# Where tiles lie in SBUF: a streaming encoder on one core, with the tiles that TensorE does not stream placed first

## The chip, the core and the metric

The kernel runs on one core of a Trainium2 chip. The metric is the device time of one execution in microseconds (us). The core has a matrix engine (TensorE, PE in the profile; its weight loads are PEld), three engines for elementwise work (VectorE is DVE, ScalarE is ACT, GpSimd is POOL) and queues that start DMA transfers (SyncE is SP). They share a scratch memory of 128 partitions, SBUF. A tile takes the same bytes of every partition, so its place is one number: the byte offset within a partition. TensorE reads two operands from SBUF for each matmul: the stationary one (128 by 128, brought in by a weight load) and the moving one (streamed through, up to 512 columns here). It writes to a separate memory, PSUM.

## The reference, cut to what matters

Input and output are 512 tokens of width 1024 in float32. The network has two layers:

```python
def reference(x, ...):
    h = x
    for layer in range(DEPTH):                      # DEPTH = 2
        if layer == N_A_LAYERS:                     # 1
            k_nope, k_rope, v = mla_shared_kv(h, ...)
        hn = rms_norm(h, mix_pre_g[layer])
        if layer < N_A_LAYERS:
            m = conformer_conv(hn, ...)             # 1024->2048, gate, 31-tap conv, norm, 1024->1024
        else:
            m = mla_attention(hn, ..., k_nope, k_rope, v, cos, sin)
        h = h + rms_norm(m, mix_post_g[layer])
        f = squared_relu_mlp(rms_norm(h, ffn_pre_g[layer]), w_ff1[layer], w_ff2[layer])   # 1024->4096->1024
        h = h + rms_norm(f, ffn_post_g[layer])
    return h
```

Most of the arithmetic is in the matrix products of the two MLPs. The kernel forms each float32 product from three products of a reduced type (fp32r): every operand is split into a high part and a low part, and high by high, low by high and high by low are added up in PSUM.

## The kernel before, in words

**Weights.** A block of weights (128 by up to 1024 columns, 512 KB) is loaded by the SP queue into a tile of the ring `raw` (5 places of 4 KB per partition). ScalarE writes its high part into a tile of the ring `wh` (5 places of 4 KB), VectorE the low part into a tile of the ring `wl` (6 places of 4 KB). TensorE then uses `wh` and `wl`. This is `weight` (L731) and `split` (L789). The rings `raw`, `wh` and `wl` are handed out in the order of first use (`fifo=True`): a block takes whichever place came free first.

**Two kinds of product.** In `products` (L768: both `ff1` matrices, the first convolution matrix, the latents) the weights are stationary and the activations move: in the profile this reads `mm<-big,wh`, the moving tile first and the stationary tile second. In `by_tokens` (L878: second convolution matrix, attention output) and `product` within `feed_forward` (L1001: `ff2`, by Strassen's seven products) the activations are stationary and the weights move: `mm<-wh,big`. A block of `ff1` is 24 matmuls of 512 columns: 8 slices of the inner dimension, each with `wh`, `wl`, `wh` as the stationary tile.

**Activations** and everything else of 2 KB per partition are in the pool `big` (48 places) and `tmp` (5 places). The residual stream `h` (4 tiles of 4 KB), the rows of gains and biases `row` (2 places of 4 KB), the vectors `vt`, the small statistics `stat`, a scratch target `junk`, the identity matrix `ident` and the averaging matrices `col` make up the rest. TensorE also reads `h` and `stat` (as stationary operands in transposes and in broadcasts), `ident` and `col` (as moving operands), in float32 and 128 columns at a time.

**Order of the work.** The program is recorded first and then scheduled by a planner (`Program`, L284) with a cost table in nanoseconds. The planner knows tiles by their ring and place number. It knows nothing of addresses.

**Addresses.** A place of a ring gets its address when its tile is first made (`Tag.make`, L208). `Tag.__init__` makes place 0 at once, where the ring is declared; the other places are made when the first instruction that uses them is issued, after planning. So in the kernel before, place 0 of every ring and all single tiles come first, in the order of their declarations, and places 1 and up follow in the order of use.

Of the kernel before, what the change touches and what calls it, by code (L numbers as in the profile page):

```python
# [8 lines left out]
F32 = mybir.dt.float32  # L9
# [5 lines left out]
P = 128  # L15
T = 512
D = 1024
# [4 lines left out]
TB = T // P  # L22
# [22 lines left out]
NVEC = _n  # L45
# [598 lines left out]
def trunk(ctx: ExitStack, tc: tile.TileContext, xT, xN, wts, vec, along, rope, cw, out):  # L644
# [6 lines left out]
    def tag(name, n, shape, where=pool, fifo=False):  # L651
        tags.append(Tag(where, name, n, shape, fifo))
        return tags[-1]

    def one(name, shape):
        return nc.tile(tag(name, 1, shape))

    RAW = tag("raw", 5, [P, D], fifo=True)
    WH = tag("wh", 5, [P, D], fifo=True)
    WL = tag("wl", 6, [P, D], fifo=True)  # L660
    BIG = tag("big", 48, [P, T])
    TMP = tag("tmp", 5, [P, T])
    MM = tag("mm", 6, [P, T], psum, fifo=True)
    BC = tag("bc", 2, [P, T], psum, fifo=True)
    STAT = tag("stat", 8, [P, 24])
    ROW = tag("row", 2, [P, D])

    JUNK = one("junk", [P, T])

    def big(dt=F32):  # L670
        return nc.tile(BIG, dt)
# [5 lines left out]
        return nc.tile(TMP)  # L677


    vt = one("vt", [P, NVEC])  # L680
    n = VEC["mix_pre0"] + KT
    nc.scalar.dma_start(out=vt[:, :n], in_=vec[:, :n])
    nc.sync.dma_start(out=vt[:, n:], in_=vec[:, n:])
# [12 lines left out]
    for k in range(KT):  # L696
        nc.sync.dma_start(out=xf[k], in_=xT[k])

    h = [one(f"h{b}", [P, D]) for b in range(TB)]
    ident = one("ident", [P, P])  # L700
    nc.gpsimd.memset(ident, 0.0)
    done = nc.gpsimd.affine_select(
        out=ident, in_=ident, compare_op=ALU.not_equal, fill=1.0, base=0, pattern=[[-1, P]], channel_multiplier=1
# [27 lines left out]
    def weight(key):  # L731

        while key not in blocks:
            name, parts = USE[len(blocks)]
            i, n = BLK[parts[0][0]], _cols[BLK[parts[0][0]]]
            if name[0] in GAINS:
                blocks[name] = scaled(name, wts[i])
                continue
            raw, hi, lo = nc.tile(RAW), nc.tile(WH, F32R), nc.tile(WL, F32R)
            step = 256 if i < 2 else n  # L740
            for o in range(0, n, step):
                nc.sync.dma_start(out=raw[:, o : o + step], in_=wts[i, :, o : o + step])
            for other, sign in parts[1:]:
                if sign > 0:
                    nc.gpsimd.dma_start(out=raw, in_=wts[BLK[other]], accum_op=ALU.add)
                else:
                    second = nc.tile(RAW)
                    nc.sync.dma_start(out=second, in_=wts[BLK[other]])
# [96 lines left out]
    def sums(parts, t0, dim):  # L845


        sm = nc.tile(BC)
        for i, (o, src, b) in enumerate(parts):

            nc.tensor.matmul(
                sm[:, o * P : (o + 1) * P], lhsT=src[:, t0 + b * P : t0 + (b + 1) * P], rhs=cols[dim],
                start=(i == 0), stop=(i == len(parts) - 1),
            )
        return sm.rearrange("p (o k) -> p o k", k=P)[:, :, 0]

    def rsqrt_bc(accs, t0, n, dim, eps, dst=None):

        nb = n // P
        sm = sums([(b, acc, b) for acc in accs for b in range(nb)], t0, dim)  # L860
        st = nc.tile(STAT)
        var = st[:, :nb]
# [8 lines left out]
    def row(name):  # L871
        t = nc.tile(ROW)
        nc.early = 30000.0
        nc.sync.dma_start(out=t, in_=along[ROWS.index(name)])
        nc.early = 0.0
        return t
# [28 lines left out]
    def residual(F, g, b, dh, o, st, on, r2):  # L905


        nc.scalar.activation(
            JUNK, F[b][dh], AF.Square, scale=1.0 / 32 if r2 is None else r2[:, b : b + 1], accum_out=st[:, o : o + 1]
        )  # L910
# [21 lines left out]
    def prenorm(X, g, t, r=None):  # L932

        t0, n = t
        for kk in range(KT // 2):
# [5 lines left out]
            for j in range(2):  # L941
# [4 lines left out]
                else:  # L946
                    split_scaled(pt, v(g, k), src, X[k], d)
        st = nc.tile(STAT)
        for i, b in enumerate(HALVES[t]):
            for dh in range(2):  # L950
                o = 16 + 2 * i + dh
                nc.scalar.activation(
                    JUNK, h[b][:, dh * DH : (dh + 1) * DH], AF.Square, scale=1.0 / 32, accum_out=st[:, o : o + 1]
                )
# [108 lines left out]
    def post_norm(gen, F, g, then, groups, r2=None, last=False):  # L1063
# [3 lines left out]
        for b, dh in gen:  # L1067
            bs = group[b]
            if not seen[bs]:
                st[bs] = nc.tile(STAT)  # L1070
            if last:
# [121 lines left out]
    for c in range(KT):  # L1193
# [29 lines left out]
        if c == 5:  # L1223

            hold = h + [nc.tile(ROW)]
            for b, t in enumerate(hold):
# [32 lines left out]
    for t0, n in (HA, HB):  # L1259
        s, nb = slice(t0, t0 + n), n // P  # L1260
        nc.scalar.activation(sq[:, s], CO[last][:, s], AF.Square)
        sm = sums([(o + b, a, b) for o, a in ((0, xs), (nb, acc), (0, CO[last]), (nb, sq)) for b in range(nb)], t0, D)
        st = nc.tile(STAT)
        mean, d2, var = st[:, 16 : 16 + nb], st[:, 20 : 20 + nb], st[:, 0:nb]
# [73 lines left out]
    def latent(name, g, dst, t, dim):  # L1338
# [12 lines left out]
        sm = sums([(b, acc, b) for b in range(nb)], t0, dim)  # L1351
        st = nc.tile(STAT)
        var, a = st[:, :nb], st[:, 12 : 12 + nb]
# [76 lines left out]
    nc.scalar.activation(undealt(r1n, FULL), dealt(r1), AF.Copy)  # L1430
    st = nc.tile(STAT)
    var, r = st[:, :TB], st[:, 16 : 16 + TB]
# [263 lines left out]
```

## Time and profile before

| what | value |
|---|---|
| time, 3 runs | 1065.81 us median (1065.62 to 1068.2) |
| span of the profiled execution | 1066.7 us, 0.9 us above that median |
| PE busy | 1045.5 us (98%), 5284 matmuls |
| PEld, DVE, ACT, POOL busy | 884.7, 764.1, 640.9, 141.6 us |
| DMA | 204.08 MB, mean 191 GB/s |
| granted TensorE clock, mean over the span | 0.993 |

A line of groups of instructions reads: source line, engine, operation, tile written, tiles read, partitions by elements and type, count, then the busy time in us and the mean duration of one in ns, then the time that the engine was idle before them and what ended it. Nearly all instructions stand at L640, the one line that issues what the planner has ordered; the tile names tell them apart. A view of stages has for each stretch its length, the busy time of each engine with the number of its instructions, the granted clock, the mean busy share of the DMA engines and what they moved. Successive matmuls overlap, so the duration of one is longer than the time from the start of one to the start of the next.

The profile does not show addresses. They are in the built program, and its matmuls stand in the same order as the trace's 5284 records, so each record can be given the addresses of its two operands. The offsets in the built program before, below 76 KB (bytes within a partition; the first 16 KB are the DMA queues' scratch area):

```
     0  DMA scratch (16384)    37088  junk (2048), 39136 vt (1460), 40608 warm
 16512  raw  place 0 (4096)    40640  h (4 tiles of 4096)
 20608  wh   place 0 (4096)    57024  ident, col (3), meanmat (512 each)
 24704  wl   place 0 (4096)    59584  uu (3 tiles of 2176)
 28800  big  place 0 (2048)    66112  r2, wq (16 each)
 30848  tmp  place 0 (2048)    66208  big (2048)
 32896  stat place 0 (96)      68256  raw (4096)
 32992  row  place 0 (4096)    72352  big (2048), and so on
```

The other places of `raw`, `wh`, `wl`, `big` and `tmp` and the second `row` lie above 65536 (64 KB): `wh` at 96928, 148128, 168608, 180896; `wl` at 109216, 154272, 162464, 172704, 176800.

### The profile page before, as it was taken

Reading aid. Unit: us, or ns where it says so; the run is one execution under the profiler, and the core shown is the slowest. Engines: PE = TensorE matmul, PEld = TensorE weight load, DVE = VectorE, ACT = ScalarE, POOL = GpSimd, SP = SyncE. Lnnn points to the kernel's source line nnn. Section 1 sums busy time; section 2 is a strip of 40 time slices with the busy share of each in tenths; the row PEclk is TensorE's granted clock in tenths of the full one; section 3 lists DMA queues with packets and bytes.
Section 4 is the critical chain, followed back from the end, with each engine's and each line's share of the span. In section 5 each row is a group of like instructions: output and inputs, shape, how many; then the busy total and the mean of one; then the engine's idle time right before and its main releaser. Section 6 shows DMA issues by size and latency. Waiting matters only on the chain. (4 is left out here: it accounts for less than half of the span.)

```text
span 1066.7 us, 15181 instructions
## 1 busy us (share of the span) xinstructions
PE 1045.5 (98%) x5284; PEld 884.7 (83%) x5284; DVE 764.1 (72%) x1559; ACT 640.9 (60%) x1343; POOL 141.6 (13%) x165
## 2 busy tenths in 40 slices
PE   8989999999999999999999999999999999999996
PEld 7878988988888888888888888889888888888885
DVE  6497994857438737959988987547574495497698
ACT  8543497766545446545767877558565554454652
POOL 1110011100100100001104533301010010000010
PEclk9989999999999999999999999999999999999998
DMA  9995888657866848658923132557599388485684
GB/s 288 300 254 171 287 211 236 156 168 207 253 171 190 257 126 241 189 182 227 237 69 93 56 100 81 174 182 179 161 245 253 112 235 257 143 243 168 187 237 129
DMA packets 67613, 204.08 MB, mean 191 GB/s; under 512 B 7632, under 2 KB 13904, under 8 KB 67536
## 3 DMA queue, kind: packets, MB, share of 16 engines
q1 hardware_dynamic: 49680, 150.15, 40.9%
q0 software_dynamic: 13536, 49.29, 25.6%
q10 hardware_dynamic: 4320, 3.68, 1.1%
q8 instruction: 41, 0.67, 0.3%
q14 instruction: 36, 0.29, 0.1%
HBM read 197.58 MB, written 5.51 MB: 190 GB/s over the span
## 5 line engine op out<-in xcount | busy, mean ns | idle before, releaser
L640 PE MATMUL mm<-big,wh 128*128 128x512 f32 (+1 forms) x1512 | 441.1, 374 | 1.2 <-ACT wh L640 1.2
L640 PE MATMUL mm<-wh,big 128*128 128x512 f32 (+1 forms) x1216 | 374.7, 387 | 0.0
L640 ACT ACTIVATE wh<-raw 128x512 fp32r<-128x512 f32 (+2 forms) x444 | 251.0, 612 | 117.7 <-PE mm L640 73.8
L640 PEld LDWEIGHTS mm<-big,wh 128*128 128x128 f32 x1512 | 275.6, 188 | 52.4 <-ACT wh L640 1.5
L640 DVE TENSOR_TENSOR wl<-raw,wh 128x512 fp32r<-128x512 f32 (+1 forms) x356 | 227.7, 680 | 106.5 <-ACT wh L640 104.1
L640 PE MATMUL mm<-big,wl 128*128 128x512 f32 (+1 forms) x756 | 282.5, 374 | 0.0
L640 PEld LDWEIGHTS mm<-wh,big 128*128 128x128 f32 x1216 | 226.3, 188 | 46.9
L640 PE MATMUL mm<-wl,big 128*128 128x512 f32 (+1 forms) x608 | 234.9, 387 | 0.1
L640 PEld LDWEIGHTS mm<-big,wl 128*128 128x128 f32 x756 | 142.6, 189 | 25.7 <-DVE wl L640 0.5
L640 PEld LDWEIGHTS mm<-wl,big 128*128 128x128 f32 x608 | 114.2, 188 | 23.4 <-DVE wl L640 0.2
L640 POOL DMA_DIRECT2D raw<-wts x64 | 55.5, 867 | 572.7 <-DMA raw<-wts 190.4
L640 ACT ACTIVATE big<-tmp 128x256 f32<-128x256 f32 (+1 forms) x208 | 95.9, 493 | 43.2 <-DVE tmp L640 37.3
L640 DVE TENSOR_TENSOR big<-big,big 128x512 f32<-128x512 f32 (+4 forms) x103 | 69.8, 698 | 55.9 <-ACT big L640 55.6
L640 ACT ACTIVATE tmp<-mm 128x512 f32<-128x512 f32 (+1 forms) x75 | 41.7, 556 | 103.1 <-PE mm L640 102.0
L640 PE MATMUL mm<-big,big 128*128 128x256 f32 (+3 forms) x520 | 83.5, 310 | 1.8 <-DVE big L640 1.8
L640 PEld LDWEIGHTS mm<-big,big 128*128 128x128 f32 x520 | 73.1, 189 | 7.0 <-DVE big L640 2.3
L640 ACT ACTIVATE big<-mm 128x512 f32<-128x512 f32 (+5 forms) x106 | 56.6, 537 | 33.9 <-PE mm L640 32.9
L640 DVE TENSOR_TENSOR big<-tmp,big 128x512 fp32r<-128x512 f32 (+1 forms) x96 | 60.9, 642 | 15.3 <-ACT big L640 12.7
L640 DVE SCALAR_TENSOR_TENSOR big<-big,vt,big 128x512 fp32r<-128x512 f32 (+29 forms) x95 | 63.3, 736 | 8.0 <-ACT big L640 8.0
L640 DVE TENSOR_TENSOR big<-big,mm 128x512 f32<-128x512 f32 x96 | 63.7, 683 | 3.2 <-PE mm L640 2.8
L640 DVE TENSOR_TENSOR tmp<-big,big 128x512 f32<-128x512 f32 x80 | 53.3, 686 | 8.9 <-ACT big L640 8.9
L640 POOL DMA_DIRECT2D wl<-wts x30 | 26.1, 869 | 213.0 <-ACT wl L640 113.3
(90 smaller groups left out, 775.9 us busy)
## 6 DMA issues: line engine op xcount, KB each, us to landing
raw<-wts SPq DMA_DIRECT2D x222, 512.0 KB, 5.0
raw<-wts POOLq DMA_DIRECT2D x64, 512.0 KB, 7.9
wl<-wts POOLq DMA_DIRECT2D x30, 512.0 KB, 8.4
big<-cw SPq DMA_DIRECT2D x45, 256.0 KB, 5.6
big<-wts SPq DMA_DIRECT2D x12, 256.0 KB, 4.3
row<-along SPq DMA_DIRECT2D x5, 512.0 KB, 5.5
raw<-wts SPq DMA_DIRECT2D x12, 192.0 KB, 2.7
big<-xT SPq DMA_DIRECT2D x8, 256.0 KB, 4.2
```

The lines of the kernel that those rows point to most:

```text
L640: return f(*args, **kwargs)
```

## The change

The declarations are put in another order, and all places of `raw` and `row` are made at once. After it the built program has, from the bottom:

```
     0  DMA scratch (16384)    47232  h (4 tiles of 4096)
 16512  raw  place 0 (4096)    63616  vt (1460)
 20608  row  place 0 (4096)    65088  stat place 0 (96)
 24704  raw  places 1 to 4     65184  ident (512)
 41088  row  place 1           65696  wh place 0, 69792 wl place 0
 45184  junk (2048)            73888  big place 0, 75936 tmp place 0
```

`col`, `meanmat`, `uu` and every place of `wh`, `wl`, `big` and `tmp` are above 65536 now. The built programs have the same instructions in the same order on every engine, with the same shapes, ring places and semaphores; addresses alone differ. The second half of the diff takes the old declarations out.

```diff
     RAW = tag("raw", 5, [P, D], fifo=True)
+    ROW = tag("row", 2, [P, D])
+    for t in (RAW, ROW):
+        for place in range(1, t.count):
+            t.make(f"{t.name}_", F32, place)
+    JUNK = one("junk", [P, T])
+    h = [one(f"h{b}", [P, D]) for b in range(TB)]
+    vt = one("vt", [P, NVEC])
+    STAT = tag("stat", 8, [P, 24])
+    ident = one("ident", [P, P])
     WH = tag("wh", 5, [P, D], fifo=True)
     WL = tag("wl", 6, [P, D], fifo=True)
     BIG = tag("big", 48, [P, T])
     TMP = tag("tmp", 5, [P, T])
     MM = tag("mm", 6, [P, T], psum, fifo=True)
     BC = tag("bc", 2, [P, T], psum, fifo=True)
-    STAT = tag("stat", 8, [P, 24])
-    ROW = tag("row", 2, [P, D])
-
-    JUNK = one("junk", [P, T])
...
-    vt = one("vt", [P, NVEC])
...
-    h = [one(f"h{b}", [P, D]) for b in range(TB)]
-    ident = one("ident", [P, P])
```

## The prediction

> **What bounds the kernel now.** I read the page's busy times first, then the stages, then what the matrix engine waits for.
>
> ```profile
> span 1066.7 us, 15181 instructions
> ...
> PE 1045.5 (98%) x5284; PEld 884.7 (83%) x5284; DVE 764.1 (72%) x1559; ACT 640.9 (60%) x1343; POOL 141.6 (13%) x165
> ```
>
> ```profile
> 0.00:50.00 50.00, 47.20 (x205) 38.55 (x206) 28.08 (x52) 33.86 (x63) 6.78 (x22) 1.00 0.98 293
> 50.00:100.00 50.00, 46.31 (x228) 39.66 (x227) 42.00 (x64) 23.09 (x48) 5.18 (x6) 0.93 0.84 226
> ...
> 250.00:300.00 50.00, 50.00 (x221) 41.09 (x220) 28.10 (x46) 30.87 (x59) 6.04 (x7) 1.00 0.90 245
> 300.00:350.00 50.00, 50.00 (x220) 41.03 (x219) 33.34 (x55) 28.30 (x56) 3.45 (x4) 1.00 0.63 178
> ```
>
> ```profile
> PE mm L640 <- DMA uu<-dealt: 3.7, 1, 3.7
> PE mm L640 <- DVE big L640: 1.8, 3, 0.7
> PE mm L640 <- POOL big L640: 1.6, 1, 1.6
> PE bc L640 <- DVE big L640: 1.5, 3, 0.7
> PE mm L640 <- ACT wh L640: 1.2, 1, 1.2
> ```
>
> In the MLP stages (two of them above) TensorE is busy 50.00 of 50.00 us: the next matmul is always ready, and the stage lasts as long as its matmuls take to follow each other. Its waits are few: 3.7 us once for a DMA, and 1.2 us in all for split weights. So the pace of the matmuls is the time, and an edit that moves no instruction can act only through that pace, or by making another engine or the DMAs slow enough to be waited for. The matmuls that carry the load are 512 columns wide:
>
> ```profile
> L640 PE MATMUL mm<-big,wh 128*128 128x512 f32 x1256 | 394.7, 393 | 1.2 <-ACT wh L640 1.2
> L640 PE MATMUL mm<-wh,big 128*128 128x512 f32 x1152 | 361.1, 392 | 0.0
> L640 PE MATMUL mm<-big,wl 128*128 128x512 f32 x628 | 246.3, 392 | 0.0
> L640 PE MATMUL mm<-wl,big 128*128 128x512 f32 x576 | 225.9, 393 | 0.0
> ```
>
> That is 3612 of the 5284. The question is whether they all follow each other at one pace. Four successive blocks of `ff1`, 24 matmuls each, cut at their first matmuls:
>
> ```profile
> 963.59:969.14 5.55, 5.55 (x25) 4.50 (x24) 5.55 (x10) 1.16 (x2) 0.86 (x1) 1.00 0.55 206
> 969.14:974.74 5.60, 5.60 (x25) 4.50 (x24) 5.60 (x11) 3.16 (x6) 0.00 (x0) 1.00 0.84 187
> 974.74:980.19 5.45, 5.45 (x25) 4.51 (x24) 4.36 (x8) 3.29 (x7) 0.00 (x0) 1.00 0.26 92
> 980.19:985.63 5.44, 5.44 (x25) 4.51 (x24) 1.90 (x3) 2.88 (x6) 0.00 (x0) 1.00 0.40 142
> ```
>
> They don't: the same work, TensorE never idle, the clock at 1.00, and 5.55, 5.60, 5.45, 5.44 us. By the built program the first block has `wl` in place 0 (offset 24704) and `wh` higher up; the second has `wh` in place 0 (20608) and `wl` higher up; the third and fourth have both above 64 KB. A change of pace within one stretch, at the matmul, in the timeline (start, duration):
>
> ```profile
> 1000.14 0.39 PE L640 MATMUL mm<-big,wl 128*128 128x512 f32 x1
> 1000.37 0.61 PE L640 MATMUL mm<-big,wh 128*128 128x512 f32 x2
> 1000.82 0.39 PE L640 MATMUL mm<-big,wl 128*128 128x512 f32 x1
> 1001.05 0.61 PE L640 MATMUL mm<-big,wh 128*128 128x512 f32 x2
> 1001.50 0.39 PE L640 MATMUL mm<-big,wl 128*128 128x512 f32 x1
> 1001.73 0.63 PE L640 MATMUL mm<-big,wh 128*128 128x512 f32 x2
> 1002.20 0.40 PE L640 MATMUL mm<-big,wl 128*128 128x512 f32 x1
> 1002.43 0.63 PE L640 MATMUL mm<-big,wh 128*128 128x512 f32 x2
> 1002.89 0.39 PE L640 MATMUL mm<-big,wl 128*128 128x512 f32 x1
> 1003.13 0.63 PE L640 MATMUL mm<-big,wh 128*128 128x512 f32 x2
> 1003.59 0.40 PE L640 MATMUL mm<-big,wl 128*128 128x512 f32 x1
> ```
>
> Three matmuls take 0.68 us up to the `wl` at 1001.50, and 0.70, 0.69, 0.70 us from there. At 1001.96, by the program, a block begins that has both `wh` and `wl` in place 0. Paired over the whole trace, record by record with the program's addresses, the 3594 steps from one fp32r matmul of 512 columns to the next that are no stall (under 300 ns) read:
>
> ```
> step from one 512-column matmul to the next     steps   median   mean
> its own or the next one's operand below 64 KB    1097   233 ns   232.39 ns
> none, but one within three matmuls                535   227 ns   228.72 ns
> none near                                        1962   227 ns   227.39 ns
> the same between 256-column matmuls: below 64 KB   184   118 ns   119.39 ns; none near 436, 120 ns, 124.81 ns
> ```
>
> It makes no difference which operand lies low: with the moving one alone low in both of two successive matmuls the mean is 232.1 ns (84 steps), with the stationary one alone 233.9 ns (218 steps). Only three tiles make up nearly all of the first row: `wh`, `wl` and `big`, place 0, at 20608 to 30848. Steps whose moving tile starts at 66208, just above 64 KB, are at the fast pace (53 steps, mean 227.1 ns).
>
> **The change part by part.** *The streamed tiles leave the lowest 64 KB.* Of the 512-column matmuls 726 read at least one such tile (474 `wh`, 203 `wl`, 47 `big`, 2 `meanmat`); the ring sizes say nearly the same, (1256 + 1152) / 5 + (628 + 576) / 6 = 682 for the weights. The gain: 1097 × (232.39 − 227.39) = 5.5 us for the steps that touch one, and 535 × (228.72 − 227.39) = 0.7 us for their neighbours, 6.2 us. The lower bound leaves the neighbours out, 5.5. The upper bound takes as the fast pace not the 227.39, which includes steps at the borders of blocks and of smaller matmuls, but the last block above, 5.44 / 24 = 226.7 ns: 1097 × 5.7 + 535 × 2.0 = 7.3 us. I take 6.2. The blocks agree: 0.11 us for `wl` alone (8 of 24 matmuls), 0.16 for `wh` alone (16 of 24), so 10 to 14 ns for each matmul that touches, and 726 × 10 = 7.3 as well.
>
> The 256-column steps show no penalty, and the float32 ones of 128 columns cost 109 to 112 ns in the median with the moving tile low or high; both count nothing.
>
> *What does not reach the end.* Up to 67 us the pace is not TensorE's alone: DMA engines are 0.98 busy in the first 50 us, and the one long wait ends at 67.3 us with a DMA (`uu<-dealt`, 3.7 us above). About 0.4 us of the gain falls before it, by the same pairing. The transfer is started by work that follows TensorE, so some of it would arrive earlier, but it queues behind loads that do not; the bounds are 0 and 0.4, and I take 0.4 as lost. After that the waits in the table are each for an engine that works on TensorE's own results, so they move with it.
>
> *All `raw` and `row` places and `h` share the lowest 64 KB.* ScalarE and VectorE read `raw`, and the DMAs write it. Before, one place of five was low, so the price is in the trace, paired the same way:
>
> ```
>                                               tile low              tiles high
> ACT wh<-raw 512 columns, raw low or high      620 ns (58)           617 ns (276)
> DVE wl<-raw,wh 512 columns, raw low or high   685.5 ns (46)         685 ns (188)
> load of raw, 512 KB, issue to landing         5.07 us (45 loads)    4.43, 5.12, 5.48, 5.17 us by place (42 to 46 loads each)
> ```
>
> (medians, counts in brackets, `wh` and `wl` high). The 3 ns of ScalarE times its 444 splits is 1.3 us of an engine that is 60% busy and 28 to 31 us of 50 in the stages above; it lies beside TensorE and the sum has 0 for it. The cover is the ring: TensorE waited 1.2 us for ScalarE's `wh` in the whole run. Without that cover the 1.3 us would be the price; I keep it in the range.
>
> *Sum.* −6.2 + 0.4 = −5.8 us: 1066.7 becomes 1060.9 for the profiled execution. That execution is 0.9 us above the median of the runs, so the time is 1065.8 − 5.8 = 1060.0 us. The ends: −7.3 with nothing lost, 1058.5; −5.5 + 0.4 + 1.3 = −3.8, 1062.0.
>
> **The rivals.** *No change (chance 0.08): 1065.8 us.* The slow steps go with something that keeps company with the three tiles, not with where they lie, and it goes with them to 65696 and up, where they now begin. For it: all three are place 0 of their ring, so address and place number are not told apart by them. Against it: in the planner a place is only a number, an address at 66208 is fast, and the slow pace holds for moving and stationary tiles, for three kinds of tile and in all stages. A page speaks for this rival: the Trainium skill, "SBUF — State Buffer", section "Who interferes with whom", says that the only contention on the engines' side is the port pair that VectorE and GpSimd share and that TensorE never waits on anyone; by that rule a tile's place could not matter and the time would stay at 1065.8. This case's trace does not agree, by the 232.39 against 227.39 ns above.
>
> *The gain is caught by the weights (0.05): about 1062.8 us.* Where loads pace the stage, faster matmuls only wait longer for `wh`. The stretch 250 to 300 us has DMA engines 0.90 busy. If half of the stretches were so close to their supply, half of the gain would go: −3. Against it stands the 1.2 us of waiting for `wh`, in one single wait.
>
> *Slower (0.04): about 1070 us.* One mechanism: all 512 KB loads now land in one 64 KB region, where ScalarE and VectorE read at the same time. If that made loads slower, the first 67 us, with DMA engines 0.98 busy, would stretch by as much. It decides from 5.8 / 67 = 9% on; at 15% it adds 10 us, 1060.0 + 10 = 1070. For it: a fifth of the loads landed there before, all of them do now, so the trace has no case of full concentration. Against it: the low place's loads took 5.07 us, amid the others, and ScalarE's reads there cost 3 ns.
>
> **How the numbers follow.** The forecast has 0.83. The range takes its bounds, 1058.5 to 1062.0, and some 0.7 us below and 1.2 us above for what the runs shown differ by (0.2 us between the two lowest, 2.4 us to the highest) and for the third case: 1057.8 to 1063.2. It leaves out the no-change and the slower case, 0.12. A measurement of this kernel can tell about 0.3% from no change, 3.2 us. Faster by more than that: the forecast and a part of the third case, 0.84; within it: no change, the rest of the third case and the forecast's upper tail, 0.12; slower 0.04.
>
> **What would show it.** Right: the 512-column steps are at 226 to 228 ns in nearly all blocks of `ff1`, each 5.44 to 5.46 us, whatever ring place they have; the means of the four groups fall from 392 to 393 towards 390 ns; PE busy falls by about 6 us while the MLP stages keep 50.00 of 50.00; the wait for `uu<-dealt` is 3.7 to 4.2 us. Wrong: some blocks still take 5.55 to 5.60 us (no change), PE's waits for `wh` grow from 1.2 us to several (caught by the weights), or the median time of the `raw` loads from issue to landing rises, with waits on DMA in the first 70 us (slower). The forecast also fails if the half-speed clock, which the 0.93 of the stage from 50 to 100 us shows once, comes a second time.

## The result and the profile after

Measured side by side on one chip, six executions each: the kernel before took 1064.8 us in the median (1063.29 to 1068.2), the changed one 1060.64 us (1058.01 to 1061.76). The ratio is 0.9959, with a 95% interval of 0.9943 to 0.9975, so the change gains 2.7 to 6.1 us. A repetition on another occasion is the first experiment below.

The page of the changed kernel, the span and the busy times:

```profile
span 1058.4 us, 15181 instructions
...
PE 1037.9 (98%) x5284; PEld 883.2 (83%) x5284; DVE 763.0 (72%) x1559; ACT 641.6 (61%) x1343; POOL 141.5 (13%) x165
```

TensorE is busy 7.6 us less for the same 5284 matmuls (1045.5 before), and no other engine moves by as much. The same four blocks of `ff1` that the prediction showed, and the one with both weights in place 0 (start and end, length, busy time of PE, PEld, DVE, ACT and POOL with their instructions, clock, DMA share, GB/s):

```profile
956.16:961.60 5.44, 5.44 (x26) 4.51 (x25) 5.44 (x10) 1.16 (x2) 0.00 (x0) 1.00 0.64 223
961.60:967.04 5.44, 5.44 (x26) 4.51 (x25) 5.44 (x10) 3.16 (x6) 0.86 (x1) 1.00 0.70 135
967.04:972.48 5.44, 5.44 (x26) 4.51 (x25) 4.76 (x8) 3.29 (x7) 0.00 (x0) 1.00 0.40 130
972.48:977.92 5.44, 5.44 (x26) 4.51 (x25) 1.89 (x3) 2.89 (x6) 0.00 (x0) 1.00 0.48 172
994.24:999.68 5.44, 5.44 (x26) 4.51 (x25) 4.56 (x8) 3.82 (x8) 1.73 (x2) 1.00 0.94 285
```

Before, the first four took 5.55, 5.60, 5.45, 5.44 us, and the fifth 5.60 (24 matmuls at 233.3 ns):

```profile
1001.96:1007.56 5.60, 5.60 (x26) 4.50 (x25) 4.40 (x7) 3.81 (x8) 1.72 (x2) 1.00 0.97 267
```

Now all are 5.44, whatever ring place they use. The groups of 512-column matmuls, by shape (busy us, mean ns of one, idle time before):

```profile
L640 PE MATMUL mm<-big,wh 128*128 128x512 f32 x1256 | 393.8, 392 | 1.1 <-ACT wh L640 1.1
L640 PE MATMUL mm<-wh,big 128*128 128x512 f32 x1152 | 358.6, 390 | 0.0
L640 PE MATMUL mm<-big,wl 128*128 128x512 f32 x628 | 246.0, 392 | 0.0
L640 PE MATMUL mm<-wl,big 128*128 128x512 f32 x576 | 224.4, 390 | 0.0
```

The means of one, 392 to 393 ns before, fell to 390 only where the weights move; where they are stationary they stay at 392. Successive matmuls overlap, so the pace shows in the blocks, not here.

What TensorE waited for (total us, times, longest):

```profile
PE mm L640 <- DVE big L640: 1.9, 3, 0.8
PE bc L640 <- DVE h L640: 1.8, 2, 1.6
PE mm L640 <- DMA uu<-dealt: 1.6, 1, 1.6
...
PE mm L640 <- ACT wh L640: 1.1, 1, 1.1
```

The wait for `wh` did not grow. The wait for `uu<-dealt` reads 1.6 us where 3.7 stood before, and one for `h` of 1.6 us is new; the stages show a second thing of that kind, the half-speed clock, which is absent in this execution (0.93 before in the first of these rows):

```profile
50.00:100.00 50.00, 48.37 (x250) 41.09 (x249) 47.08 (x72) 23.48 (x47) 4.90 (x6) 1.00 0.84 237
...
300.00:350.00 50.00, 50.00 (x222) 41.42 (x221) 37.28 (x61) 28.50 (x56) 4.31 (x5) 1.00 0.66 181
```

Paired matmul by matmul, the two profiled executions differ by 8.2 us from first to last matmul:

```
before to after                                    up to the first matmul on uu    from there on
steps that change by no more than 60 ns (pace)               -0.35 us                -6.29 us
larger steps: waits and clock                                -0.54 us                -1.07 us
```

The pace is 6.6 us of it. Of the larger steps the biggest are the half clock before (-2.7 us, 66.3 to 73.1 us), the shorter wait for `uu` (-2.1), a longer start at half clock after (+1.5) and the wait for `h` (+1.7). The repetitions show that these come and go by themselves.

### The profile page after: what moved, and what is told of

The parts are those of the page before. It is cut to its first block, busy times and chain, and to the rows that moved or that the text cites. A ratio compares the mean times of both kernels' runs of the same rounds, so it can differ in the third digit from the quotient of the medians.

```text
span 1058.4 us, 15181 instructions
## 1 busy us (share of the span) xinstructions
PE 1037.9 (98%) x5284; PEld 883.2 (83%) x5284; DVE 763.0 (72%) x1559; ACT 641.6 (61%) x1343; POOL 141.5 (13%) x165
## 4 chain that ended last, share of the span: by engine, by line
PE 85%; DVE 7%; DMA 3%; ACT 3%; issue 1%; DVEq 0%; ACTq 0%
PE mm L640 82%; DVE big L640 5%; PE bc L640 3%; DMA raw<-wts 2%; ACT big L640 2%; DVE stat L640 1%; DVE wl L640 1%; ACT wh L640 1%; ACT wl L640 1%; DMA uu<-dealt 1%; DMA dealt<-big 1%; DVE tmp L640 0%; ACT tmp L640 0%; DVE h L640 0%; DMA vt<-vec 0%
## 5 line engine op out<-in xcount | busy, mean ns | idle before, releaser
L640 DVE TENSOR_TENSOR wl<-raw,wh 128x512 fp32r<-128x512 f32 (+1 forms) x356 | 227.2, 679 | 105.9 <-ACT wh L640 105.5
L640 PEld LDWEIGHTS mm<-big,big 128*128 128x128 f32 x520 | 73.1, 190 | 7.0 <-DVE big L640 2.4
```

What stands on the lines that cost most here:

```text
L640: return f(*args, **kwargs)
```

## The experiments

Names in the tables: "before" and "change" are the two kernels above. In every kernel below, each engine has the same instructions in the same order, with the same semaphores, as in these two; addresses alone differ.

### Both kernels again, the raw ring alone, the weights low

*The change and the kernel before, unaltered.*

> The changed kernel once more, unaltered. In the first pair of profiles the steps between matmuls beside the three low tiles gave 6.7 us; four other places moved as well: the wait for uu<-dealt at 64 us (2.1 us shorter), a half-clock stretch behind it that was there before and is gone (2.7 us), a later full clock at the start (1.6 us lost), and a wait for DVE's h at 511 us (1.7 us lost). Theory (pace alone is the change's own, the rest is chance from run to run): over five rounds the time is 5.5 to 6.7 us below the kernel before, ratio 0.9937 to 0.9948, and the profile shows the four other places differently again. Rival (the wait at 511 us is the gain caught by DVE or by the loads, in every run): 4 to 5 us, ratio 0.9953 to 0.9962, and the wait of 1.6 us for h is there again.

> The kernel before once more, for a second profile of it. Theory (chance from run to run): the wait for uu<-dealt, the half-clock stretch behind it and the start of the full clock differ from the first profile by 1 to 3 us each, while the steps beside low tiles are the same 232.4 ns to 0.2 ns and the wait for h at 518 us may or may not be there. Rival (they belong to the placement): 3.7 us of waiting for uu, 6.8 us at half clock, and no wait for h, as in the first profile.

Measured: the change 1061.16 us (1057.72 to 1062.84, 6 executions) against 1065.95 us (17 executions) for before, ratio 0.9942 with an interval of 0.9921 to 0.9962; before alone 1066.97 in its one execution. The medians are 4.8 us apart and the ratio stands for 6.2, so the time alone holds both the theory's and the rival's amount; the traces decide. Paired, this second pair of traces has a pace of -0.41 us before the first matmul on `uu` and -6.08 after it, so -6.5 where the first pair had -6.6, while its larger steps add up to +2.3 us where the first pair had -1.6. The change's own two executions differ by 0.00 us in pace and by 2.6 us in waits and clock. The stages of the repeated change show part of these 2.6 us:

```profile
50.00:100.00 50.00, 47.45 (x239) 40.63 (x238) 44.48 (x68) 22.58 (x46) 4.86 (x6) 0.97 0.84 235
100.00:150.00 50.00, 47.47 (x361) 45.09 (x360) 46.45 (x100) 29.55 (x65) 3.82 (x5) 0.97 0.78 217
```

It has two short stretches at half clock (67.8 to 71.2 and 146.3 to 149.7 us), and the step that waits for `h` is 0.6 us long where it was 2.0. The kernel before, repeated, has the same two stretches where its first execution had one of 6.8 us:

```profile
50.00:100.00 50.00, 47.97 (x240) 40.91 (x239) 44.79 (x69) 23.09 (x47) 4.90 (x6) 0.97 0.84 235
100.00:150.00 50.00, 48.07 (x370) 45.80 (x369) 47.16 (x105) 29.45 (x65) 4.31 (x5) 0.97 0.79 223
```

Its wait for `uu<-dealt` is 2.0 us instead of 3.7, its steps beside low tiles have the same mean of 232.4 ns, and the pace of its two executions differs by 0.2 us in all. So the pace belongs to the kernel, and the rest to the execution.

*The raw ring and the norm rows low, the streamed rings directly above them.* `wh`, `wl` and `big` place 0 stay in the lowest 64 KB, at 45184, 49280 and 53376.

```diff
     for t in (RAW, ROW):
         for place in range(1, t.count):
             t.make(f"{t.name}_", F32, place)
-    JUNK = one("junk", [P, T])
-    h = [one(f"h{b}", [P, D]) for b in range(TB)]
-    vt = one("vt", [P, NVEC])
-    STAT = tag("stat", 8, [P, 24])
-    ident = one("ident", [P, P])
     WH = tag("wh", 5, [P, D], fifo=True)
...
     BC = tag("bc", 2, [P, T], psum, fifo=True)
+    JUNK = one("junk", [P, T])
+    h = [one(f"h{b}", [P, D]) for b in range(TB)]
+    vt = one("vt", [P, NVEC])
+    STAT = tag("stat", 8, [P, 24])
+    ident = one("ident", [P, P])
```

> One part of the change alone: all raw and row places go to the lowest 64 KB, but place 0 of wh, wl and big stays there too (45184, 49280, 53376); 724 of the 512-column matmuls read a low tile, as before. Theory (where raw lies costs nothing): the kernel before, within 1 us, ratio 0.999 to 1.001, and raw loads land in 4.4 to 5.5 us by place. Rival (loads that all land in one region are slower): slower than before by some us, with a higher share of DMA time and longer landings in the first 70 us. Rival (raw in one region helps): faster than before by 1 us or more.

Measured: 1064.82 us (10 executions), ratio 0.9989 (0.9978 to 1.0001). All raw loads land in one region and nothing slows down. The DMA issues of this kernel's page (count, size, median us from issue to landing) are the same as before's 5.0 and 7.9 us:

```profile
raw<-wts SPq DMA_DIRECT2D x222, 512.0 KB, 5.0
raw<-wts POOLq DMA_DIRECT2D x64, 512.0 KB, 7.9
```

The rival "slower" falls, and the raw ring has no part in the faster pace either: the steps have the means of the kernel before (table below). The median is 1.1 us below before's, at the edge of what was expected, and the interval includes no change.

*The weights low.* All places of `wl` and three of the five of `wh` in the lowest 64 KB (one more lies across its end), raw and all activations above.

```diff
-    RAW = tag("raw", 5, [P, D], fifo=True)
+    WL = tag("wl", 6, [P, D], fifo=True)
     ROW = tag("row", 2, [P, D])
-    for t in (RAW, ROW):
+    for t in (WL, ROW):
         for place in range(1, t.count):
             t.make(f"{t.name}_", F32, place)
     JUNK = one("junk", [P, T])
+    WH = tag("wh", 5, [P, D], fifo=True)
+    for t in (WH,):
+        for place in range(1, t.count):
+            t.make(f"{t.name}_", F32, place)
+    RAW = tag("raw", 5, [P, D], fifo=True)
+    BIG = tag("big", 48, [P, T])
+    TMP = tag("tmp", 5, [P, T])
...
     h = [one(f"h{b}", [P, D]) for b in range(TB)]
     vt = one("vt", [P, NVEC])
     STAT = tag("stat", 8, [P, 24])
     ident = one("ident", [P, P])
-    WH = tag("wh", 5, [P, D], fifo=True)
-    WL = tag("wl", 6, [P, D], fifo=True)
-    BIG = tag("big", 48, [P, T])
-    TMP = tag("tmp", 5, [P, T])
...
```

> The opposite placement: all six wl places (16512 to 45184), three of five wh places (51328, 55424, 59520) lie below 65536, one wh place straddles it (63616), one is above (67712); raw, h, vt, stat and all but place 0 of nothing else are above. By the program's addresses 2894 of the 512-column matmuls read a low tile, against 726 before and none in the change; 3310 steps touch one, 268 lie near one. Theory (any operand below 64 KB costs the step, wherever below, and whatever else lives there): 17 to 19 us slower than the change, so 11 to 13 us slower than before, ratio to before about 1.011; ff1 blocks with wh and wl low take 5.60 us. In the straddling wh tile the slow steps end with the slice at 65536. Rival (the slow tiles contend with raw, h, vt and stat, which share the low 64 KB in the kernel before): with these moved out, the low weights run at 226.7 ns and the time equals the change. Rival (only the region 20 to 31 KB is slow): the wh places at 51 to 62 KB run fast, and the cost is a third of it, about 6 us above the change.

Measured: 1078.52 us (1077.3 to 1079.27), ratio 1.0113 (1.0096 to 1.013). The direction speaks for the 64 KB. The blocks don't quite (the same four blocks of `ff1`):

```profile
970.52:976.11 5.59, 5.59 (x25) 4.50 (x24) 5.59 (x10) 1.15 (x2) 0.86 (x1) 1.00 0.51 192
976.11:981.71 5.60, 5.60 (x25) 4.50 (x24) 5.60 (x11) 3.16 (x6) 0.00 (x0) 1.00 0.77 187
981.71:987.31 5.60, 5.60 (x25) 4.50 (x24) 4.27 (x7) 3.29 (x7) 0.00 (x0) 1.00 0.26 91
```

In the third block only `wl` lies below 64 KB (8 of its 24 matmuls); before, such a block took 5.55 us. Here it takes the full 5.60, as if its `wh`, above the line, were slow too.

### Where exactly the line is

*All of `wl` low, all of `wh` above (69760 to 86144).*

```diff
+    WL = tag("wl", 6, [P, D], fifo=True)
+    for t in (WL,):
+        for place in range(1, t.count):
+            t.make(f"{t.name}_", F32, place)
     RAW = tag("raw", 5, [P, D], fifo=True)
...
+    WH = tag("wh", 5, [P, D], fifo=True)
+    for t in (WH,):
+        for place in range(1, t.count):
+            t.make(f"{t.name}_", F32, place)
+    BIG = tag("big", 48, [P, T])
+    TMP = tag("tmp", 5, [P, T])
...
     JUNK = one("junk", [P, T])
     h = [one(f"h{b}", [P, D]) for b in range(TB)]
...
     STAT = tag("stat", 8, [P, 24])
     ident = one("ident", [P, P])
-    WH = tag("wh", 5, [P, D], fifo=True)
-    WL = tag("wl", 6, [P, D], fifo=True)
-    BIG = tag("big", 48, [P, T])
-    TMP = tag("tmp", 5, [P, T])
...
```

> All six wl places low (16512 to 41088), all five wh places above 64 KB (69760 to 90240), activations above. Each product of three then has one low tile in the middle. In the kernel before, such a block among fast ones steps at 235, 232, 227 ns, 231.3 on average; in the run with nearly all weights low, blocks with wh at 67712 and a low wl stepped at 233.4 ns throughout, though two of three matmuls had no low tile. Theory A (a low tile costs the step that leads to it and the one that follows, 13 ns in all, and nothing further): every ff1 block at 231.3 ns, 1204 low matmuls x 13 ns = 15.7 us of pace above the change, 13 to 15 us in time. Theory B (an address near 67 to 71 KB counts as low too, the border is above 64 KB): blocks with wh at 69760 at 233.3, those with wh from 73856 up at 231.3. Theory C (once slow, the stream stays slow as long as a low tile comes at least every third matmul): all blocks at 233.3 ns, about 22 us of pace, 17 to 20 us in time.

Measured: 1077.37 us (1076.97 to 1077.78), ratio 1.0108 (1.0077 to 1.0139). Every block has 8 low matmuls of 24 and takes 233.3 ns a matmul, 5.60 us, as theory C has it:

```profile
970.58:976.18 5.60, 5.60 (x26) 4.50 (x25) 5.60 (x10) 1.15 (x2) 0.86 (x1) 1.00 0.48 185
976.18:981.78 5.60, 5.60 (x26) 4.50 (x25) 5.60 (x11) 3.17 (x6) 0.00 (x0) 1.00 0.77 187
```

*`wh` place 0 across the line (63616 to 67712), `wl` place 0 above it at 67712.*

```diff
     h = [one(f"h{b}", [P, D]) for b in range(TB)]
-    vt = one("vt", [P, NVEC])
-    STAT = tag("stat", 8, [P, 24])
-    ident = one("ident", [P, P])
     WH = tag("wh", 5, [P, D], fifo=True)
...
     BC = tag("bc", 2, [P, T], psum, fifo=True)
+    vt = one("vt", [P, NVEC])
+    STAT = tag("stat", 8, [P, 24])
+    ident = one("ident", [P, P])
```

> The change, but wh place 0 lies across 65536 (63616 to 67712; weight slices 0 to 2 below, 3 across, 4 to 7 above) and wl place 0 at 67712; all else streamed is above. Theory (the border is at 65536 and is sharp): in the 12 ff1 blocks with this wh place the first 9 to 12 steps are slow (231 to 236 ns) and the last 12 are 227 ns, a block costs about 0.08 us, not 0.16; wl at 67712 is fast. Rival (the border is higher, 72 KB or so): these blocks are slow to the end, and so are those with wl at 67712. In all 3 us of pace above the change.

Measured: 1070.13 us, one execution. The same four blocks:

```profile
965.21:970.76 5.55, 5.55 (x25) 4.51 (x25) 5.55 (x10) 1.16 (x2) 0.79 (x1) 1.00 0.54 204
970.76:976.36 5.60, 5.60 (x25) 4.51 (x25) 5.60 (x10) 3.16 (x6) 0.07 (x1) 1.00 0.76 186
976.36:981.81 5.45, 5.45 (x25) 4.49 (x25) 4.42 (x8) 3.30 (x7) 0.00 (x0) 1.00 0.24 94
```

The pattern of the kernel before, unchanged (the paces of all its steps are the same too, and the 3 us by which this execution is longer than most of before lie in its waits and clock). But the first block's `wl` now lies wholly above 64 KB, at 67712, and in the second block the slow pace lasts to its end, although the last four of the eight slices of `wh` lie above the line. The rival of a higher line foresaw both, but in the change `wh` at 65696 and `wl` at 69792 are fast. A line at 64 KB, or at any one address, can't do that.

*Activations low:* `big` places 0 to 22 in the lowest 64 KB, weights above.

```diff
+    BIG = tag("big", 48, [P, T])
+    for place in range(1, 23):
+        BIG.make("big_", F32, place)
+    ROW = tag("row", 2, [P, D])
     RAW = tag("raw", 5, [P, D], fifo=True)
-    ROW = tag("row", 2, [P, D])
-    for t in (RAW, ROW):
-        for place in range(1, t.count):
-            t.make(f"{t.name}_", F32, place)
+    WH = tag("wh", 5, [P, D], fifo=True)
+    WL = tag("wl", 6, [P, D], fifo=True)
+    TMP = tag("tmp", 5, [P, T])
...
     JUNK = one("junk", [P, T])
...
     ident = one("ident", [P, P])
-    WH = tag("wh", 5, [P, D], fifo=True)
-    WL = tag("wl", 6, [P, D], fifo=True)
-    BIG = tag("big", 48, [P, T])
-    TMP = tag("tmp", 5, [P, T])
...
```

> The activations instead of the weights: 23 of the 48 places of big lie below 64 KB (16512 to 63616), all wh, wl and tmp places above. 1067 of the 512-column matmuls have a low moving tile, 756 others a low stationary one; 2381 steps touch one. Theory (any fp32r operand below 64 KB, moving or stationary, whichever tile it is): steps with the moving tile low at 231 to 235 ns, 13 to 15 us of pace above the change, 9 to 13 us in time, ratio to before 1.005 to 1.008. Rival (it belongs to the weight tiles, which ScalarE and VectorE have just written, not to the place): the time of the change, ratio 0.995.

Measured: 1072.51 us (1071.92 to 1073.57), ratio 1.0063 (1.0042 to 1.0084). Both operands can cause the slow pace, as the prediction's pairing had it; this run alone tells no cause.

What the slow tiles of these kernels do share is the last digits of their offsets. (Two tiles are said to agree within N bytes if their offsets leave the same remainder on division by N.) In the kernel before, all tiles declared ahead of `stat`, which has 96 bytes, start at a multiple of 128 (16512, 20608, 24704, 28800); every later place of the streamed rings starts 32 bytes past one (66208, 96928, 148128 and so on). In the change, `vt`, `stat` and `ident` are declared ahead of `wh`, so that all places of these rings start 32 bytes past a multiple of 128. In the run across the line, 63616 and 67712 are multiples of 128, and so on through all slow tiles. The move out of the lowest 64 KB and this shift came together.

### Three offsets

The theory was now that a start at a multiple of 64 bytes is slow in itself. Its rivals: the lowest 64 KB after all, and that only a *pair* of tiles with different offsets is slow. Unused tiles of a few bytes move the rings without anything else.

*Low, but at 32:* the kernel before with

```diff
+    pool.tile([P, 8], F32, tag="pad0", name="pad0", bufs=1)
     RAW = tag("raw", 5, [P, D], fifo=True)
...
     ident = one("ident", [P, P])
+    pool.tile([P, 8], F32, tag="pad1", name="pad1", bufs=1)
```

> The kernel before with two unused tiles of 32 bytes a partition, one before the raw ring and one after the identity, and nothing else. The first place of high parts, low parts and big tiles still lies in the lowest 64 KB (at 20640, 24736 and 28832), but now every streamed tile starts 32 bytes past a multiple of 64. Theory now (a tile that starts at a multiple of 64 bytes is slow, wherever it lies): the steps of 512 columns around these three places fall from 231 to 235 ns to 227 ns, all ff1 blocks take 226.7 ns a matmul, and the time is that of the change, 1059 to 1062 us (ratio 0.994 to 0.997). Rival (what lies in the lowest 64 KB is slow, the prediction's theory): the steps stay at 231 to 235 ns and the time is the kernel before's, ratio 0.999 to 1.001.

Measured: 1064.67 us (12 executions), ratio 0.9991 (0.9978 to 1.0004): no gain, so a start at a multiple of 64 is not what is slow. The time is the one that the 64 KB would give, but the run across the line has ruled these out already. The blocks:

```profile
961.66:967.21 5.55, 5.55 (x26) 4.52 (x25) 5.55 (x10) 1.16 (x2) 0.63 (x1) 1.00 0.54 202
967.21:972.74 5.53, 5.53 (x26) 4.51 (x25) 5.53 (x10) 3.16 (x6) 0.23 (x1) 1.00 0.78 187
972.74:978.20 5.46, 5.46 (x26) 4.50 (x25) 4.44 (x8) 3.29 (x7) 0.00 (x0) 1.00 0.26 96
```

Here the low places lie 32 past a multiple of 128, and all others, pushed on by two unused tiles, 96 past one: again two kinds of offset.

*The change with all streamed tiles at multiples of 128* (an unused tile of 96 bytes ahead of `wh`):

```diff
     ident = one("ident", [P, P])
+    pool.tile([P, 24], F32, tag="pad0", name="pad0", bufs=1)
     WH = tag("wh", 5, [P, D], fifo=True)
```

> The change with one unused tile of 96 bytes a partition made just before the ring of high parts: every streamed tile lies above the lowest 64 KB as in the change, but starts at a multiple of 128 bytes instead of 32 past one. Theory now (a start at a multiple of 64 is slow in itself): every step of 512 columns at 233.3 ns instead of 227, which over some 3,600 such steps is 22 us of pace, of which 5 to 7 us come back from waits for transfers as in the runs with slow weights: 1075 to 1079 us, ratio to before 1.009 to 1.013. Rival 1 (slow is only a pair of tiles that start at different offsets within 64 bytes; here all agree): 227 ns and 1059 to 1062 us. Rival 2 (the lowest 64 KB are slow): also 1059 to 1062 us.

*And at 64 past a multiple of 128* (the same with `[P, 8]`):

> The same with the unused tile at 32 bytes, so that every streamed tile starts 64 bytes past a multiple of 128. Theory now with a period of 64 bytes: as with multiples of 128, 233.3 ns a step and 1075 to 1079 us. With a period of 128 bytes: 227 ns and 1059 to 1062 us. Lowest 64 KB or unequal offsets: 1059 to 1062 us.

Measured: 1060.62 us (ratio 0.9956, 0.9941 to 0.9971) and 1060.07 us (0.9943, 0.9926 to 0.996). Both are as fast as the change; the theory is wrong a second time. The blocks of the first:

```profile
955.53:960.97 5.44, 5.44 (x26) 4.50 (x25) 5.44 (x10) 1.16 (x2) 0.57 (x1) 1.00 0.59 213
960.97:966.41 5.44, 5.44 (x26) 4.50 (x25) 5.44 (x10) 3.16 (x6) 0.29 (x1) 1.00 0.81 187
```

*The change with `wh` at 96 and `wl`, `big` at 32*, all above 64 KB:

```diff
     ident = one("ident", [P, P])
+    pool.tile([P, 16], F32, tag="pad0", name="pad0", bufs=1)
     WH = tag("wh", 5, [P, D], fifo=True)
+    for place in range(1, 5):
+        WH.make("wh_", F32, place)
+    pool.tile([P, 16], F32, tag="pad1", name="pad1", bufs=1)
```

> The change with the ring of high parts made early between two unused tiles of 64 bytes, so that the high parts start 96 bytes past a multiple of 128 and the low parts and big tiles 32 past one. With a period of 64 bytes these are equal: 226.7 ns a step, the span of the change, 1057 to 1062 us. If two offsets within 128 bytes must agree, or 96 is slow in itself: steps with high parts (half of all) at about 233 ns, 1066 to 1070 us.

Measured: 1072.08 us, one execution, with nothing that TensorE streams below 64 KB. The time is above both of the ranges expected. Its blocks are at neither of the two known paces (with moving weights, in the other products, the steps have a mean of 233.2 ns):

```profile
966.10:971.63 5.53, 5.53 (x26) 4.51 (x25) 5.53 (x11) 1.16 (x2) 0.86 (x1) 1.00 0.52 187
971.63:977.13 5.50, 5.50 (x26) 4.51 (x25) 5.50 (x11) 3.16 (x6) 0.00 (x0) 1.00 0.79 191
```

An offset of 96 is not slow in itself: in the first of these four runs, steps among tiles at 96 alone have a mean of 227.2 ns. These four leave the pair: fast is every kernel whose streamed tiles all have one offset within 128 bytes (0, 32 or 64), slow are those with two.

### Low, and all alike

The last run puts this against the 64 KB directly, and asks within how many bytes the offsets must agree:

```diff
     RAW = tag("raw", 5, [P, D], fifo=True)
+    pool.tile([P, 8], F32, tag="pad0", name="pad0", bufs=1)
     WH = tag("wh", 5, [P, D], fifo=True)
+    pool.tile([P, 32], F32, tag="pad1", name="pad1", bufs=1)
     WL = tag("wl", 6, [P, D], fifo=True)
+    pool.tile([P, 32], F32, tag="pad2", name="pad2", bufs=1)
     BIG = tag("big", 48, [P, T])
     TMP = tag("tmp", 5, [P, T])
+    pool.tile([P, 56], F32, tag="pad3", name="pad3", bufs=1)
```

> The kernel before with four unused tiles among its rings (32, 128, 128 and 224 bytes), so that the first places of the streamed rings stay in the lowest 64 KB (high parts at 20640, low parts at 24864, big tiles at 29088) but all streamed tiles agree in their offset within 128 bytes (32). Against the other places, the first place of the high parts agrees within 512 bytes, that of the low parts only within 128 bytes, that of the big tiles within 256 but not 512. Theory now (a step is slow where the tiles that it streams differ in their offset within 128 bytes): every step of 512 columns at 226.8 to 227 ns, 1059 to 1062 us, ratio 0.994 to 0.997. Offsets within a longer stretch: the steps with the first place of low parts (and of big tiles, for 512) stay at 230 to 234 ns, those with the first place of high parts fall to 227; 1061 to 1064 us. The prediction's theory (the lowest 64 KB are slow wherever a tile starts): all three stay at 231 to 235 ns, ratio 0.999 to 1.001.

Measured: 1060.89 us (1059.7 to 1062.14), ratio 0.996 (0.9946 to 0.9974), the time of the change, with `wh`, `wl` and `big` place 0 in the lowest 64 KB. By the time alone 128 bytes could be enough; the blocks tell: `wl` place 0 in the first, `wh` place 0 in the second, neither in the third, both in the last:

```profile
957.88:963.43 5.55, 5.55 (x26) 4.54 (x25) 5.55 (x10) 1.15 (x2) 0.59 (x1) 1.00 0.65 224
963.43:968.87 5.44, 5.44 (x26) 4.51 (x25) 5.44 (x10) 3.16 (x6) 0.28 (x1) 1.00 0.83 190
968.87:974.31 5.44, 5.44 (x26) 4.51 (x25) 4.59 (x8) 3.30 (x7) 0.00 (x0) 1.00 0.28 84
...
996.07:1001.62 5.55, 5.55 (x26) 4.54 (x25) 4.52 (x8) 3.81 (x8) 0.87 (x2) 1.00 0.93 276
```

The second block took 5.60 us before and takes 5.44 at nearly the same low address, 20640 for 20608: the lowest 64 KB cost nothing. The first keeps its 5.55: `wl` place 0 agrees with the rest only within 128 bytes (288 against 160, within 512). `big` place 0 (416 against 160) agrees within 256 bytes, and its 77 steps free of other causes have a mean of 226.9 ns. So 128 bytes are not enough, 256 are, and 512 aren't needed.

All kernels in one table: steps between 512-column fp32r matmuls under 260 ns, with nothing but such matmuls for three on either side (so 1046 for the kernel before, not the 1097 of the prediction), sorted by whether the operands of a matmul and of the next all have one offset within 256 bytes ("equal", and so for three matmuls on either side) or not (those between are left out), and the time from the first matmul on `uu` to the last matmul.

```
kernel                     apart by   unequal: steps, mean    equal: steps, mean    uu at    from there to the end
before                        32        1046   232.42 ns       1905   226.95 ns     67.3       989.4 us
raw ring low                  32        1046   232.43          1905   226.96        65.8       986.9
wh across 64 KB               32        1044   232.42          1905   227.00        66.6       991.8
weights low                   32        3364   233.32             7   -             65.1      1000.4
wl low                        32        3361   233.32             7   -             65.8       999.8
activations low               32        2522   232.58           164   228.45        65.3       995.4
low, but at 32                64        1044   230.94          1905   227.20        65.5       989.0
wh at 96, rest at 32          64        3377   231.15            12   -             64.9       995.4
low and alike (wl: 128)      128         376   231.95          2655   226.80        66.8       983.6
change                         -           4   -               3378   226.83        66.4       982.0
change again                   -           4   -               3382   226.82        66.5       984.6
all at 0                       -           4   -               3376   226.81        65.0       982.7
all at 64                      -           4   -               3373   226.83        66.4       983.6
```

The 376 of the last run's row hold 97 that are not slow (told below). The 164 equal steps with the activations low have 228.45 ns, which these runs leave unexplained.

## Why the prediction was right, and where it was wrong

**The number and the size of the gain.** Forecast was 1060.0 us, in a range of 1057.8 to 1063.2; measured 1060.64 and 1061.16. As a difference, 5.8 us were forecast, and the medians moved by 4.2 and 4.8; the intervals (2.7 to 6.1, and by 0.9921 to 0.9962 4.1 to 8.4 us) hold the forecast. The term of the pace, 6.2 us with ends of 5.5 and 7.3, measured 6.6 and 6.5 in the two pairs of traces. The last ff1 block as the measure of the fast pace, 226.7 ns, held for every block: 5.44 us is what each of the five blocks shown takes now. That the time came within 0.6 us is in part luck: the median of before was 1.0 us lower side by side than the 1065.8 it was counted from, while the difference was 1.6 us smaller than forecast.

**What does not reach the end.** 0.4 us were taken as lost ahead of `uu<-dealt`; the pairing has 0.35 and 0.41 there, and the column "uu at" bears it out as far as it can: that matmul starts at 64.9 to 67.3 us in kernels of every pace, the slowest (65.1 us with the weights low) no later than the fastest. Behind that point the two executions of before need 989.4 us each and the two of the change 982.0 and 984.6, and the pace alone (6.1 to 6.3) lies between these differences of 7.4 and 4.8. The waits move by 1 to 3 us from one execution to the next; the half clock, which the prediction had named as a way to fail, came twice in the repeated execution of each kernel, 3.4 us long each time, and the time stayed in the range (1062.81 us in that execution of the change). For the wait on `uu<-dealt` the prediction named 3.7 to 4.2 us; it reads 1.6, and 2.5 in the repetition, and since the pace before it repeats, this is the execution's and not the change's.

**What it took for the cause: wrong.** The step that failed is the first of the part on the change, "The streamed tiles leave the lowest 64 KB", with its row "below 64 KB 232.39 ns, none near 227.39 ns". The steps were slow as stated, but the region was not the reason. In the rings that make up nearly all of that row, the three tiles were the only ones whose offsets differ from the others' by 32 bytes within 256, and the change made these offsets alike, by declaring the 96 bytes of `stat` and the 1460 of `vt` ahead of the rings; the single tiles still behind them add up to a multiple of 256. Nobody aimed at that: as far as the cause goes, the right number is luck, since the same move out of the lowest 64 KB with two kinds of offset gains nothing (the run with `wh` at 96, 1072.08 us in its one execution). The last run shows it on both sides: 668 steps that touch a tile below 64 KB with offsets alike within 256 bytes have a mean of 226.7 ns, 376 with unlike offsets 231.95 ns, in one execution.

**The rival "no change" was half right,** and the prediction gave it 0.08. It said that the slow steps go with something that keeps company with the three tiles, which is so; it went on that this would follow them to 65696, which is not. What was brought against it, a fast address just above the line (66208), could not decide: 66208 agrees with all the other fast tiles within 256 bytes, so it was fast for the second reason too. The pairing had separated the moving from the stationary operand, but hardly ever two low tiles from each other, nor high tiles of another offset: the kernel before has only four matmuls with both operands low, each beside unlike ones, and no high place of these rings with another offset. The Trainium skill, "SBUF — State Buffer", section "Who interferes with whom", by whose rule TensorE never waits on anyone, would have had no change; the time disagrees with what the prediction derived from it, 1065.8 us. These runs do not test the rule as one between engines: what slows the steps is the relation of TensorE's own two operands, and no other engine's work changed. The Trainium skill, "SBUF — State Buffer", section "Operand start alignment", treats the start of an operand as a matter of what is legal and says that its runs "timed nothing"; here the starts of TensorE's two operands against each other are worth 6 ns in 227.

**The other rivals.** "Slower", by loads crowded in one region, is refuted by the raw ring low on its own, 0.9989, with unchanged landing times. "The gain is caught by the weights": the wait for `wh` stayed at 1.1 us, against 1.2. In the other direction something is given back: with the weights low the pace adds 1.4 us before `uu` and 20.0 after, and the larger steps return 4.4 us, most of it by shorter waits (for `uu` 1.8 us, for `h` 1.4) and an earlier full clock (0.9), so that the span is 17.1 us longer than the change's. The medians, 17.4 us apart, lie below the 21.4 of the pace too; how much of this belongs to the kernel is not shown.

## What to carry to other kernels

Give all tiles that TensorE streams (moving and stationary alike) one offset within 256 bytes of each other, for instance by declaring small odd-sized tiles ahead of all rings or padding them to 256 bytes. Declared behind the rings, as in the kernel before, they come between place 0, which is made at once, and the other places, which are made later. Here it is worth 0.4 to 0.6%, and getting it wrong for all weights made the kernel 1.1% slower than before. Where a slow pace goes with an address, list the offsets' low digits beside the region before naming the region as the cause, and try pads of a few bytes between the rings: they change these digits and leave the region as it is. A difference of profiles of a few us should be split into pace and single large steps before it is explained, since here the pace repeats to 0.0 us (change) and 0.2 us (before), and the large steps vary by 1 to 3.

## What the runs showed of the hardware that was not expected

A 512-column fp32r matmul follows another in 226.8 ns where the moving and stationary tiles of both start at one offset within 256 bytes, and in 231 to 234 ns in the mean where they don't (32 bytes apart 232.4 to 233.3, 64 apart 230.9 to 231.2, 128 apart 232.4 to 234.1 where it counts). The absolute offset doesn't matter: 0, 32 and 64 past a multiple of 128 gave 226.81, 226.83 and 226.83. In the last run a low `wl` 128 bytes apart shows which relations count at that distance, a matmul's moving tile against its own stationary tile and against the next one's: as the moving tile it makes its own step slow (234.0 ns, 96 steps) and not the one before (227.1, 97 steps), as the stationary tile both the one before, in which it is loaded (232.4, 96 steps), and its own (234.1, 94 steps). At smaller distances it is not the same. At 32 bytes, in the kernel before, the step ahead of an unlike moving tile is not free: 223 steps have a mean of 230.8 ns. At 64, in the run with `wh` at 96, the step from a matched pair in which an unlike stationary tile is loaded has 227.8 ns (584 steps), and the one ahead of an unlike moving tile 235.7 (541 steps). With the weights low the stationary tiles of an `ff1` block agree and nearly all moving ones do, and the blocks are slow throughout: so it is the moving against the stationary operand, not a change from one matmul to the next. Why the two should meet at all, the runs don't show; nor was any other type, step width or engine tried on purpose. Steps between 256-column fp32r matmuls show no penalty in any of these kernels: with the weights low, 440 unlike ones have a mean of 117.5 ns, and in the change 638 alike ones 119.7.
